# An mLSTM and pooling block on one core: block sums spread over three feature tiles, the first head's loads reordered, and every store to DRAM issued by GpSimd's queue

## The chip, the core and the metric

One core of a Trainium2 chip runs the kernel. The metric is the device time of one execution in microseconds. A run also leaves a profile of one execution, whose span is the time from its first to its last instruction.

Short names: PE is TensorE, PEld its weight loads, DVE VectorE, ACT ScalarE, POOL GpSimd, SP SyncE. SPq and POOLq are the sequencers of SP and POOL, which also issue transfers. L375 is line 375 of the kernel before.

## The reference, cut to what matters

Two layers act on 1024 latent tokens of width 1024; 256 context tokens stand before them. Layer 0 is a bidirectional mLSTM over four heads of 512, layer 1 a grid pooling mixer. Cut to what the change touches:

```
h = modulate(rmsnorm(x, pre_g), shift, scale)       # latent and context
xm, z, og = split(h @ w_in, 3)                      # 2048 features each
xc = silu(short_conv(xm)); q, k = headwise(xc); v = headwise(xm)
hsum = bidir_mlstm(q, k, v, gates)                  # context states first
y = (sigmoid(og) * headnorm(hsum) + skip * xc) * silu(z) @ w_out
x = x + gate * rmsnorm(y)
u, z = split(h2 @ w_in, 2)                          # layer 1
x = x + gate * rmsnorm((pool_diff(u) @ w_pool * scale * silu(z)) @ w_out)
```

All is float32. The kernel makes each product from three matmuls, on a high and a low part of both operands, so each operand needs a split: a copy on ACT for the high part and a subtraction on DVE for the low one.

## The kernel before

**Features (`features`, `token_part`).** Sixteen tiles of 128 features, n = 0 to 15. A tile multiplies one weight tile by three chunks of tokens (512, 512, 256), eight steps of three matmuls each. Each chunk is copied out of PSUM twice on ACT (L373 into the convolution's input, L375 into the high part `xmh`), DVE makes the low part (L376). Then come the convolution (L378 on ACT, L379 and L380 on DVE, L381 on ACT) and its split (L388 ACT, L389 DVE). `token_part(n)` is a generator whose matmuls are put between those of tile n + 1, from its first chunk on; they read `xmh` of tile n. A tile stores `xc` (L383), four pieces of its split (L391, L392), and two pairs of value tiles (L421): nine stores.

**Block sums.** `block_sums` prepares, for k = 0 to 3, four sums of blocks of h for the products that follow. For one k it loads two rows of h (L519), makes four sums on DVE (L522 to L525), and for each of the four sums a split (L529 on ACT, L530 on DVE) and a store (L531). It is a generator with six yields for one k; after each feature tile from n = 2 on, three of its steps are taken (two from n = 10 on), so that one k takes two tiles: loads, sums and one split after the even tile, three splits after the odd one.

**Gates and the z and og products.** One pair of tiles is multiplied plainly, the other pairs by a block scheme of seven products (`strassen`), whose weight sums POOL makes (L575 to L578). `o_done` stores two tiles for each result (L625).

**Heads.** Four heads, eight tiles of 128 tokens each. For each tile `decay` fills tiles with exp (ACT), POOL masks their diagonals (L774, L775), `score_chunk` multiplies three chunks of keys, `weights` normalises, `turn` transposes, `values` multiplies by v (POOL takes a power in it, L814), and `store` writes 128 x 512 to DRAM (L831). Before the first tile L850 to L856 load the first head's keys by chunks (`fetch_x`), the gate rows (`load_gates`, `load_ctx_gates`, two and two transfers) and v (`fetch_v`); `next_q` makes the first queries.

**Output and layer 1.** `product` multiplies by an output weight, `residual` scales, adds and stores (L1009), partly on POOL; layer 1's `pool_tile` stores L1162. The last quarter of the tokens ends with three stores (L1207).

**What sets the order.** Every transfer, load or store, is issued by SP's queue, in order: a store that waits for its data holds the loads behind it. Each engine works through its own list in order, too. PE's order is written out by hand for the features, the z and og products, the output products and layer 1. All other orders are made by a scheduler when the program is built: it takes the instructions in program order as their priority, and plays them through against modelled durations. Buffers come from pools by tag: "S4" has 32 buffers of 4 KB a partition, "T5" 5, "hn" 3, "pt" 6. A tile waits for a free buffer of its tag, and a stored tile's buffer is free when the store has landed.

Of the kernel before, what the change touches and what calls it, by code (L numbers as in the profile page):

```python
# [51 lines left out]
def hybrid_block(ctx: ExitStack, tc: tile.TileContext, xT, ctxT, vecs, w_ada0, w_ada, w_blk, w_krow, blk_mask, w_gate, w_in, b_gate, w_out,  # L52
# [209 lines left out]
    def modulate(src, r, parts, k, j, dst=None):  # L262
        sc, sh = gs0[:, k, j:j + 1], mod0[:, k, 0, j:j + 1]
        V.scalar_tensor_tensor(src, src, sc, r, op0=ALU.mult, op1=ALU.mult)
        if dst is not None:
            nc.sync.dma_start(dst, src)
        for hi, _, c in parts:
            S.activation(hi, src[:, c], AF.Identity, bias=sh)
        for hi, lo, c in parts:
            V.scalar_tensor_tensor(lo, src[:, c], sh, f(hi), op0=ALU.add, op1=ALU.subtract)  # L270
# [87 lines left out]
    def features(n, side):  # L358
        wh, wl = first_w[n] if n < 2 else load_w(w_in[n])
        xp = tl("T5", [P, 1284])  # L360
        for z in (0, 1025, 1282):
            G.memset(xp[:, z:z + 1], 0.0)
        cp = tl("pt", [P, 2, TC], F32R)
        xmh = [tl("S4", [P, T], F32R), cp[:, 0]]
        xml = [tl("S4", [P, T], F32R), cp[:, 1]]
        for ci, (o, w) in enumerate(CHUNKS):
            p = pt_("pa") if n > 1 else ps_[n][ci]
            for k in range(KD if n > 1 else 0):
                mm3(p[:, :w], wh[:, k], wl[:, k], hx(k, ci, 0), hx(k, ci, 1), k == 0, k == KD - 1)
                if n == 2 or k % 2:  # L370
                    next(side, None)
            xo = 1 + o if ci < 2 else 1026
            S.activation(xp[:, xo:xo + w], p[:, :w], AF.Copy)  # L373
            dh, dl = (xmh[0][:, o:o + w], xml[0][:, o:o + w]) if ci < 2 else (xmh[1], xml[1])
            S.activation(dh, p[:, :w], AF.Copy)  # L375
            V.tensor_tensor(dl, xp[:, xo:xo + w], f(dh), op=ALU.subtract)  # L376
        y = tl("T5", [P, 1281])
        S.activation(y, xp[:, 1:1282], AF.Identity, scale=vc("conv_w", 16 + n), bias=vc("conv_b", n))  # L378
        V.scalar_tensor_tensor(y, xp[:, 0:1281], vc("conv_w", n), y, op0=ALU.mult, op1=ALU.add)  # L379
        V.scalar_tensor_tensor(y, xp[:, 2:1283], vc("conv_w", 32 + n), y, op0=ALU.mult, op1=ALU.add)  # L380
        S.activation(y, y, AF.Silu)  # L381
        yl, yc = y[:, 0:T], y[:, 1025:1281]
        nc.sync.dma_start(xc_d[n], yl)  # L383
        cp = tl("pt", [P, 2, TC], F32R)
        xch = [tl("S4", [P, T], F32R), cp[:, 0]]
        xcl = [tl("S4", [P, T], F32R), cp[:, 1]]
        for s_, h_, l_ in ((yl, xch[0], xcl[0]), (yc, xch[1], xcl[1])):
            S.activation(h_, s_, AF.Copy)  # L388
            V.tensor_tensor(l_, s_, f(h_), op=ALU.subtract)  # L389
        for t, dst in ((xch, xh_d), (xcl, xl_d)):  # L390
            nc.sync.dma_start(dst[n, :, 0:T], f(t[0]))  # L391
            nc.sync.dma_start(dst[n, :, T:TA], f(t[1]))  # L392
        return xmh, xml, xch, xcl

    def token_part(n, xmh, xml, xch, xcl):
# [8 lines left out]
        for s0 in (0, 5):  # L404
            vst, vhl = tl("T5", [P, 2, 5, 144]), tl("T5", [P, 2, 5, P], F32R)
            for s in range(s0, s0 + 5):
                yield
                if s < 8:
                    ah, al = xmh[0][:, s * P:(s + 1) * P], xml[0][:, s * P:(s + 1) * P]
                else:  # L410
                    ah, al = xmh[1][:, (s - 8) * P:(s - 7) * P], xml[1][:, (s - 8) * P:(s - 7) * P]
                p = pt_("pb", [P, 2, 144])
                mm(p.rearrange("p a b -> p (a b)"), ah, vv.rearrange("p a b -> p (a b)"), True, False)
                mm(p[:, 0], al, vv[:, 0], False, True)
                S.activation(vst[:, :, s - s0], p, AF.Copy)  # L415
            V.tensor_tensor(vst[:, 0], vst[:, 0], vst[:, 1], op=ALU.add)
            V.tensor_tensor(pre[:, s0:s0 + 5], pre[:, s0:s0 + 5], vst[:, 0, :, P:], op=ALU.add)
            S.activation(vhl[:, 0], vst[:, 0, :, :P], AF.Copy)
            V.tensor_tensor(vhl[:, 1], vst[:, 0, :, :P], f(vhl[:, 0]), op=ALU.subtract)
            for t, dst in ((vhl[:, 0], vh_d), (vhl[:, 1], vl_d)):  # L420
                nc.sync.dma_start(dst[n // 4, :, s0:s0 + 5, (n % 4) * P:(n % 4 + 1) * P], f(t))  # L421
        yield

        gx = gx_all[:, n]
# [13 lines left out]
    def gates():  # L438
# [56 lines left out]
        scans(m_r, mc_r, ALU.max, lambda r, a, b, st: i_r[r, a:b][:, ::st])  # L495
        V.tensor_tensor(i_r[:36, 0:T], i_r[:36, 0:T], b_r[:36], op=ALU.subtract)
        V.tensor_tensor(i_r[:36, T:TA], i_r[:36, T:TA], bc_r[:36], op=ALU.subtract)
        nc.sync.dma_start(a_d, i_r[:36, :])
        V.tensor_tensor(b_r[:36], b_r[:36], m_r[:36], op=ALU.subtract)
        yield  # L500
        nbt.append(small([P, 8, 36], "cst", 1))
# [9 lines left out]
    def block_sums():  # L511
# [4 lines left out]
        for k in range(4):  # L516
            t0, t1 = tl("S4", [P, T]), tl("S4", [P, T])
            for t, kk in ((t0, k), (t1, k + 4)):
                nc.sync.dma_start(t, h_d[kk])  # L519
            yield  # L520
            b11, b12, b21, b22 = t0[:, :512], t0[:, 512:], t1[:, :512], t1[:, 512:]
            V.scalar_tensor_tensor(b22, b22, dsh[:, k], b12, op0=ALU.add, op1=ALU.subtract)  # L522
            V.tensor_tensor(b12, b12, b11, op=ALU.subtract)
# [3 lines left out]
            for j, x in ((2, b11), (3, b22), (1, b12), (4, b21)):  # L527
                t = tl("S4", [P, 2, 512], F32R)
                S.activation(t[:, 0], x, AF.Copy)  # L529
                V.tensor_tensor(t[:, 1], x, f(t[:, 0]), op=ALU.subtract)  # L530
                nc.sync.dma_start(t_d[j - 1, k], f(t))  # L531
                yield

    side, parts, sums = iter(()), [], block_sums()
    with ctx0:
        gate_weights()
        for n in range(KE):
# [76 lines left out]
        def o_done(n, sz, xc, i, hf, t):  # L614
# [7 lines left out]
                nc.sync.dma_start(x, xc_d[n + i, :, hf * 512:hf * 512 + 512])  # L622
            V.scalar_tensor_tensor(x, x, vc("skip", n + i), sz[i][:, hf], op0=ALU.mult, op1=ALU.mult)
            for t_, dst in ((sg, ga_d), (x, gb_d)):
                nc.sync.dma_start(dst[(n + i) // 4, 4 * hf:4 * hf + 4, :, (n + i) % 4].rearrange("t p x -> p t x"),  # L625
                                  t_.rearrange("p (t x) -> p t x", t=4))

        steps = gates()
# [72 lines left out]
                hd.setdefault(part, []).append(t)  # L701

    def load_ctx_gates(h):
        rc = tl("hn", [P, 2, TC])
        for d in range(2):
            nc.sync.dma_start(rc[:, d], a_d[32 * d + h:32 * d + h + 1, T:TA].to_broadcast([P, TC]))
        return rc
# [115 lines left out]
    def store(st, tag="pc"):  # L823
# [4 lines left out]
        ht = tl("hn", [P, 4, P])  # L828
        V.tensor_tensor(ht, p, ab[0], op=ALU.mult)
        V.tensor_tensor(ht, ht, ab[1], op=ALU.add)  # L830
        nc.sync.dma_start(y1_d[4 * h:4 * h + 4, :, ti * P:(ti + 1) * P].rearrange("c p t -> p c t"), ht)  # L831

    BYTES["T5"] = 5120
    phase("ph2")
# [13 lines left out]
            fetch_x(cur["hd"], cur["h"], ci)  # L848

    cur = start_head(0)  # L850
    fetch_x(cur["hd"], 0, 1)
    cur["A"] = make_A(0)
    cur["q"] = next_q(cur, 0)
    cur["R"], cur["rc"] = load_gates(0), load_ctx_gates(0)
    fetch_x(cur["hd"], 0, 2)
    fetch_v(cur["hd"], 0, 0, 5)  # L856
    st_prev = st_now = nxt = None
    for i in range(len(seq) + 1):
# [137 lines left out]
    def residual(yo, rs, o, w, xr, dst, acc2, engs):  # L996
# [5 lines left out]
        for n in range(8):  # L1002
# [3 lines left out]
            if acc2 is not None:  # L1006
                squares(t, acc2, n, w)
            if n % per == per - 1:
                nc.sync.dma_start(dst[:, n - per + 1:n + 1, o:o + w], yo[n // per])  # L1009
            yield STEP_R * w / 512  # L1010

    gg0 = const([P, 8], "gg0")
# [100 lines left out]
    for g in range(4):  # L1113
# [32 lines left out]
        def pool_tile(j):  # L1146
            n = 4 * g + j
            w = load_w(bw_pool[n], 4)
            for hf in range(2):
# [9 lines left out]
                    o = yraw[n // 2, hf][:, n % 2]  # L1159
                V.scalar_tensor_tensor(o, p, vc("pool_scale", n), szs[j][:, s_], op0=ALU.mult, op1=ALU.mult)  # L1160
                if g < 3:
                    nc.sync.dma_start(y2_d[n, :, s_], o)  # L1162

        def box_tile(j):
            d.append(box(ut[j], g, imv))
# [36 lines left out]
    for e, i, n0, n1 in ((V, 0, 0, 4), (G, 1, 2, 4), (V, 1, 0, 2)):  # L1202
# [1 line left out]
        r = rs if e is V else rss  # L1204
        e.tensor_tensor(t, t, r[:, None, :].to_broadcast([P, n1 - n0, 256]), op=ALU.mult)
        e.tensor_tensor(t, t, xr[i][:, n0:n1], op=ALU.add)
        nc.sync.dma_start(outT[:, 4 * i + n0:4 * i + n1, 768:1024], t)  # L1207
    ph["stack"].close()


# [77 lines left out]
```

## Time and profile before

| | before |
|---|---|
| median of 3 runs | 2068.04 us (2063.6 to 2069.58) |
| the profiled execution, its own time | 2062.41 us |
| its span | 2060.7 us |
| mean granted clock of PE | 0.986 |
| PE busy | 1982.7 us, 96% of the span |
| DVE, ACT, POOL busy | 61%, 39%, 14% |
| moved by DMA | 339.47 MB, 165 GB/s over the span |

Busy times do not count the instructions that issue transfers. A wait in the tables below is the idle time of an engine in front of an instruction, with the instruction or transfer that ended it. The granted clock is a share of 2.4 GHz.

### The profile page before, as it was taken

What the parts mean: (1) busy time and instruction counts of PE and PEld (TensorE: products, weight loads), DVE (VectorE), ACT (ScalarE), POOL (GpSimd) and SP (SyncE); (2) the same over time, 40 slices, a digit from 0 to 9 for tenths busy, and PEclk for the clock granted to TensorE, in tenths of its full rate; (3) what the DMA queues carried; (4) which work ended last, traced back from release to release, by engine and by line L of the source; (5) the groups of instructions that cost most, each with busy time, mean ns of one, the idle gap of its engine ahead of it and who ended that gap; (6) DMA issues with size and microseconds to landing.
All of it is one profiled execution on the core that took longest, in us unless ns stands there. A gap on an engine that the chain in (4) does not pass through costs nothing.

```text
span 2060.7 us, 26787 instructions
## 1 busy us (share of the span) xinstructions
PE 1982.7 (96%) x10050; PEld 1668.4 (81%) x10050; DVE 1258.9 (61%) x2092; ACT 809.4 (39%) x1353; POOL 289.5 (14%) x376
## 2 busy tenths in 40 slices
PE   6888889999999999999999999999999999999997
PEld 4777778788888788888888878887888888888897
DVE  4766666787677667667576672544747283744444
ACT  5566666533333432333323322443423132224443
POOL 1000000023322100000000001343000000000275
PEclk9999999999999999999999999999999999999999
DMA  9376776864444854638346334534331312134573
GB/s 364 135 249 219 233 245 215 275 221 128 148 137 125 274 200 139 225 123 275 109 161 213 108 97 138 193 115 164 101 112 51 103 52 87 52 114 137 177 249 127
DMA packets 202499, 339.47 MB, mean 165 GB/s; under 512 B 13021, under 2 KB 116957, under 8 KB 202369
## 3 DMA queue, kind: packets, MB, share of 16 engines
q1 hardware_dynamic: 202368, 337.76, 48.8%
q8 instruction: 78, 1.28, 0.2%
q14 instruction: 53, 0.43, 0.1%
HBM read 234.77 MB, written 102.94 MB: 164 GB/s over the span
## 4 chain that ended last, share of the span: by engine, by line
PE 86%; DVE 5%; DMA 5%; ACT 2%; issue 1%; SPq 0%; POOL 0%; DVEq 0%; ACTq 0%; POOLq 0%
PE pa L136 43%; PE pc L136 34%; PE pb L136 7%; PE pb L796 1%; DMA wr<-in_w_ada_dram 1%; PE pc L827 1%; DMA S<-in_w_ada_dram 1%; DVE S L917 1%; DMA S<-in_ctxT_dram 0%; DMA vl_d<-T 0%; DVE wl L673 0%; DMA T<-in_bw_out_dram 0%; DMA S<-xh_d 0%; DMA cst<-in_w_blk_dram 0%; DVE wl L144 0%
## 5 line engine op out<-in xcount | busy, mean ns | idle before, releaser
L136 PE MATMUL pa<-S,wh 128*128 128x512 f32 (+1 forms) x2448 | 712.7, 376 | 1.7 <-ACT pt L375 1.7
L136 PEld LDWEIGHTS pa<-S,wh 128*128 128x128 f32 x2448 | 439.5, 191 | 72.2 <-ACT pt L375 2.9
L136 PE MATMUL pc<-S,wh 128*128 128x512 f32 (+1 forms) x1664 | 464.7, 365 | 3.2 <-ACT wh L142 2.3
L136 PE MATMUL pa<-S,wl 128*128 128x512 f32 (+1 forms) x1224 | 454.0, 371 | 3.3 <-DVE wl L144 3.3
L136 PEld LDWEIGHTS pc<-S,wh 128*128 128x128 f32 x1664 | 301.5, 189 | 54.6 <-ACT wh L142 2.5
L144 DVE TENSOR_TENSOR wl<-wr,wh 128x1024 fp32r<-128x1024 f32 (+1 forms) x124 | 146.9, 1185 | 267.2 <-ACT wh L142 266.0
L136 PE MATMUL pc<-S,wl 128*128 128x512 f32 (+1 forms) x832 | 302.3, 365 | 1.0 <-DVE wl L144 1.0
L136 PEld LDWEIGHTS pa<-S,wl 128*128 128x128 f32 x1224 | 233.1, 190 | 44.0 <-DVE wl L144 3.7
L142 ACT ACTIVATE wh<-wr 128x1024 fp32r<-128x1024 f32 (+1 forms) x124 | 124.6, 1005 | 358.1 <-PE pa L136 137.0
L136 PE MATMUL pa<-S,S 128*128 128x512 f32 (+1 forms) x1152 | 249.0, 362 | 5.4 <-DMA S<-xh_d 5.0
L136 PE MATMUL pc<-S,pt 128*128 128x512 f32 x960 | 227.5, 391 | 1.4 <-DVE S L736 0.9
L136 PEld LDWEIGHTS pa<-S,S 128*128 128x128 f32 x1152 | 191.7, 190 | 34.8 <-DMA S<-xh_d 5.5
L136 PEld LDWEIGHTS pc<-S,pt 128*128 128x128 f32 x960 | 178.2, 188 | 38.4 <-DVE S L736 1.6
L136 PEld LDWEIGHTS pc<-S,wl 128*128 128x128 f32 x832 | 157.5, 189 | 26.4 <-DVE wl L144 1.8
L798 ACT ACTIVATE pt<-pb 128x512 fp32r<-128x512 f32 (+1 forms) x96 | 47.8, 524 | 211.8 <-PE pb L796 202.7
L985 POOL TENSOR_TENSOR hn<-hn,pt 128x512 f32<-128x512 f32 (+1 forms) x48 | 77.7, 1621 | 308.4 <-ACT pt L984 307.4
L755 DVE SCALAR_TENSOR_TENSOR T<-pa,T 128x256 f32<-128x256 f32 (+3 forms) x184 | 78.1, 453 | 35.9 <-PE pa L136 31.4
L136 PEld LDWEIGHTS pb<-vv,S 128*128 128x128 f32 x256 | 48.3, 194 | 40.3 <-ACT S L375 16.2
L415 ACT ACTIVATE T<-pb 128x288 f32<-128x288 f32 x160 | 62.9, 412 | 43.2 <-PE pb L136 42.7
L585 ACT ACTIVATE wh<-T 128x512 fp32r<-128x512 f32 x70 | 41.2, 626 | 98.3 <-PE pc L136 79.6
L136 PE MATMUL pb<-S,wh 128*128 128x512 f32 x256 | 78.8, 389 | 0.0
L136 PE MATMUL pb<-vv,S 128*128 128x288 f32 (+1 forms) x256 | 50.1, 276 | 27.0 <-ACT S L375 14.5
(323 smaller groups left out, 2340.8 us busy)
## 6 DMA issues: line engine op xcount, KB each, us to landing
wr<-in_bw_in_dram SPq DMA_DIRECT2D x40, 512.0 KB, 3.5
wr<-in_w_in_dram SPq DMA_DIRECT2D x34, 512.0 KB, 4.3
wr<-in_w_ada_dram SPq DMA_DIRECT2D x32, 512.0 KB, 3.8
wr<-in_w_out_dram SPq DMA_DIRECT2D x32, 512.0 KB, 3.6
T<-in_bw_out_dram SPq DMA_DIRECT2D x32, 512.0 KB, 4.7
S<-y_d SPq DMA_DIRECT2D x28, 512.0 KB, 7.5
vh_d<-T SPq DMA_DIRECT2D x32, 320.0 KB, 2.8
vl_d<-T SPq DMA_DIRECT2D x32, 320.0 KB, 3.6
```

The costliest lines, as they stand in the source:

```text
L136: PE.matmul(out, lhsT, rhs, start=start, stop=stop)
L142: S.activation(h, r, AF.Copy)
L144: V.tensor_tensor(l, r, f(h), op=ALU.subtract)
L415: S.activation(vst[:, :, s - s0], p, AF.Copy)
L585: S.activation(hi, a, AF.Copy)
L755: V.scalar_tensor_tensor(W[:, lo + sh:hi + sh], p[:, lo - o:hi - o], 1.0, W[:, lo + sh:hi + sh], op0=ALU.mult, op1=ALU.mult, accum_out=dp[ ...
L796: PE.transpose(p[:, j], st["M"][:, s * P:(s + 1) * P], ident)
L798: S.activation(th[:, :n], p[:, :n], AF.Copy)
L827: PE.transpose(p[:, c], hn[:, c * P:(c + 1) * P], ident)
L917: V.tensor_tensor(b, yraw[kp, hf], f(a), op=ALU.subtract)
L985: G.tensor_tensor(acc, acc, sq, op=ALU.add)
```

## The change

The diff has three parts. All stores to DRAM (306 of them by the loops of the code: 8 of h, 16 + 64 of the convolution's results, 64 value tiles, 1 of gate rows, 16 block sums, 64 gates, 32 + 8 + 24 intermediate results, 9 outputs) are issued by `nc.gpsimd` instead of `nc.sync`; loads stay on SP. `block_sums` yields three times for one k instead of six, and one step is taken after each tile from n = 2 on: loads and sums after one tile, two splits after the next, two after the third. For the first head, all gate rows and keys are loaded ahead of `make_A` and `next_q`, and its context gate rows lie in an "S4" buffer instead of an "hn" one.

```
@@ stores, 14 places, all alike
-            nc.sync.dma_start(dst, src)
+            nc.gpsimd.dma_start(dst, src)
@@ block_sums
             for t, kk in ((t0, k), (t1, k + 4)):
                 nc.sync.dma_start(t, h_d[kk])
-            yield
             b11, b12, b21, b22 = t0[:, :512], t0[:, 512:], t1[:, :512], t1[:, 512:]
...
                 V.tensor_tensor(t[:, 1], x, f(t[:, 0]), op=ALU.subtract)
-                nc.sync.dma_start(t_d[j - 1, k], f(t))
-                yield
+                nc.gpsimd.dma_start(t_d[j - 1, k], f(t))
+                if j in (3, 4):
+                    yield
...
             if n >= 2:
-                for _ in range(3 if n < 10 else 2):
-                    next(sums, None)
+                next(sums, None)
@@ load_ctx_gates
-        rc = tl("hn", [P, 2, TC])
+        rc = tl("hn" if h else "S4", [P, 2, TC])
@@ first head
     cur = start_head(0)
-    fetch_x(cur["hd"], 0, 1)
+    cur["R"], cur["rc"] = load_gates(0), load_ctx_gates(0)
+    finish_x(cur)
     cur["A"] = make_A(0)
     cur["q"] = next_q(cur, 0)
-    cur["R"], cur["rc"] = load_gates(0), load_ctx_gates(0)
-    fetch_x(cur["hd"], 0, 2)
     fetch_v(cur["hd"], 0, 0, 5)
```

## Rows read from the trace of the kernel before

**Rows 1.** The page, its span and part 1: busy time, share, instructions.
```profile
span 2060.7 us, 26787 instructions
...
PE 1982.7 (96%) x10050; PEld 1668.4 (81%) x10050; DVE 1258.9 (61%) x2092; ACT 809.4 (39%) x1353; POOL 289.5 (14%) x376
```

**Rows 2.** Busy time by engine in four stretches; last columns clock, DMA share, GB/s.
```profile
core 0: us, PE busy (x) PEld busy (x) DVE busy (x) ACT busy (x) POOL busy (x), PEclk, DMA share, GB/s
115.20:292.10 176.90, 153.54 (x788) 127.36 (x788) 115.88 (x181) 109.47 (x203) 2.11 (x25) 0.92 0.70 239
309.64:379.72 70.08, 70.08 (x393) 59.81 (x393) 46.44 (x68) 48.98 (x94) 0.49 (x9) 1.00 0.66 211
703.00:723.00 20.00, 14.96 (x71) 12.35 (x69) 10.12 (x22) 12.47 (x23) 2.04 (x7) 0.91 1.04 362
1984.00:2004.00 20.00, 16.92 (x127) 16.52 (x127) 7.11 (x6) 7.21 (x11) 10.29 (x8) 0.92 1.01 352
```

**Rows 3.** PE's waits, whole span: us in total, times, longest us.
```profile
PE pb L136 <- ACT S L375: 14.5, 4, 4.0
...
PE pa L136 <- DMA S<-xh_d: 5.0, 1, 5.0
```

**Rows 4.** Timeline around a feature tile with block sums, 205 to 236 us.
```profile
215.98 0.97 SPq L519 DMA_DIRECT2D S<-h_d  x1
...
222.65 0.75 DVE L522 SCALAR_TENSOR_TENSOR S<-S,dsh,S 128x512 f32<-128x512 f32 x1 [0.17 <-DMA S<-h_d]
...
227.24 0.63 ACT L529 ACTIVATE S<-S 128x512 fp32r<-128x512 f32 x1 [3.49 <-DVE S L524]
227.77 1.07 ACT L375 ACTIVATE S<-pa 128x512 fp32r<-128x512 f32 x2
228.40 0.19 PEld L136 LDWEIGHTS pb<-vv,S 128*128 128x128 f32 x1 [3.98 <-ACT S L375]
228.40 0.40 PE L136 MATMUL pb<-vv,S 128*128 128x288 f32 x1 [3.56 <-ACT S L375]
```

**Rows 5.** Timeline of a feature tile without block sums, 298 to 317 us.
```profile
298.15 0.60 ACT L373 ACTIVATE T<-pa 128x512 f32<-128x512 f32 x1 [1.02 <-PE pa L136]
...
301.93 0.62 ACT L375 ACTIVATE S<-pa 128x512 fp32r<-128x512 f32 x1
...
308.34 0.17 POOL L362 MEMSET T<- 128x1 f32 x3 [18.12 <-DVE vv L402]
...
315.68 0.60 ACT L373 ACTIVATE T<-pa 128x512 f32<-128x512 f32 x1 [1.01 <-PE pa L136]
```

**Rows 6.** Groups by line on DVE, 115.2 to 292.1 us: busy us, mean ns.
```profile
L416 DVE TENSOR_TENSOR T<-T 128x720 f32<-128x720 f32 x16 | 14.4, 903 | 8.4 <-ACT T L415 8.4
...
L530 DVE TENSOR_TENSOR S<-S,S 128x512 fp32r<-128x512 f32 x16 | 10.3, 684 | 0.0
...
L522 DVE SCALAR_TENSOR_TENSOR S<-S,dsh,S 128x512 f32<-128x512 f32 x4 | 3.0, 752 | 1.0 <-DMA vl_d<-T 0.6 <-DMA S<-h_d 0.4
```

**Rows 7.** Groups by line and form on POOL, whole span.
```profile
L577 POOL TENSOR_TENSOR T<-wr,T 128x512 f32<-128x512 f32 x14 | 23.3, 1661 | 145.5 <-DVE wl L586 143.5 <-PE pb L504 2.0
L576 POOL TENSOR_TENSOR T<-T,wr 128x512 f32<-128x512 f32 x14 | 18.6, 1328 | 1.0
```

**Rows 8.** Line 421's issues on SP: duration ns min/median/max, and landing.
```profile
L421 SPq DMA_DIRECT2D vh_d<-T x32: 359/370/1050, 100.1 to 396.2; - x32
...
DMA to landing us min/median/max: 2.4/3.2/9.2
```

**Rows 9.** Timeline at the start of the heads, 700 to 712 us.
```profile
705.14 1.07 ACT L735 ACTIVATE S<-pc 128x512 fp32r<-128x512 f32 x2
...
705.68 0.39 SPq L713 DMA_DIRECT2D S<-a_d  x1
...
708.33 0.67 SPq L686 DMA_DIRECT2D S<-xh_d  x1
...
711.34 0.99 ACT L770 ACTIVATE T<-S,cst 128x128 f32<-128x128 f32 x3 [3.83 <-DMA S<-a_d]
```

**Rows 10.** The chain that ended last, 700 to 724 us: start, us, what.
```profile
708.33 8.92 DMA S<-xh_d
```

**Rows 11.** Timeline in the last output product, 1976 to 2006 us.
```profile
1979.61 7.04 POOL L1005 TENSOR_TENSOR S<-S,S 128x512 f32<-128x512 f32 x4
...
1986.67 0.38 SPq L1009 DMA_DIRECT2D out_dram<-S  x1
...
1988.54 13.01 SPq L140 DMA_DIRECT2D T<-in_bw_out_dram  x7
```

**Rows 12.** Timeline of the last 15 us.
```profile
2053.85 2.61 DVE L1206 TENSOR_TENSOR S<-S,S 128x1024 f32<-128x1024 f32 x2
2054.80 2.05 SPq L1207 DMA_DIRECT2D out_dram<-S  x3
```

**Rows 13.** Timeline of one tile in the heads, 990 to 1026 us.
```profile
1000.99 0.81 DVE L816 TENSOR_SCALAR hn<-pc,mv,rs__1597_9027 128x512 f32<-128x512 f32 x1 [0.73 <-POOL rs__1597_9027 L814]
```

More of the change, by code (lines that the diff above doesn't have):

```diff
@@ L382, in features @@
         yl, yc = y[:, 0:T], y[:, 1025:1281]
-        nc.sync.dma_start(xc_d[n], yl)
+        nc.gpsimd.dma_start(xc_d[n], yl)
         cp = tl("pt", [P, 2, TC], F32R)
@@ L390, in features @@
         for t, dst in ((xch, xh_d), (xcl, xl_d)):
-            nc.sync.dma_start(dst[n, :, 0:T], f(t[0]))
-            nc.sync.dma_start(dst[n, :, T:TA], f(t[1]))
+            nc.gpsimd.dma_start(dst[n, :, 0:T], f(t[0]))
+            nc.gpsimd.dma_start(dst[n, :, T:TA], f(t[1]))
         return xmh, xml, xch, xcl
@@ L420, in token_part @@
             for t, dst in ((vhl[:, 0], vh_d), (vhl[:, 1], vl_d)):
-                nc.sync.dma_start(dst[n // 4, :, s0:s0 + 5, (n % 4) * P:(n % 4 + 1) * P], f(t))
+                nc.gpsimd.dma_start(dst[n // 4, :, s0:s0 + 5, (n % 4) * P:(n % 4 + 1) * P], f(t))
         yield
@@ L497, in gates @@
         V.tensor_tensor(i_r[:36, T:TA], i_r[:36, T:TA], bc_r[:36], op=ALU.subtract)
-        nc.sync.dma_start(a_d, i_r[:36, :])
+        nc.gpsimd.dma_start(a_d, i_r[:36, :])
         V.tensor_tensor(b_r[:36], b_r[:36], m_r[:36], op=ALU.subtract)
@@ L624, in o_done @@
             for t_, dst in ((sg, ga_d), (x, gb_d)):
-                nc.sync.dma_start(dst[(n + i) // 4, 4 * hf:4 * hf + 4, :, (n + i) % 4].rearrange("t p x -> p t x"),
+                nc.gpsimd.dma_start(dst[(n + i) // 4, 4 * hf:4 * hf + 4, :, (n + i) % 4].rearrange("t p x -> p t x"),
                                   t_.rearrange("p (t x) -> p t x", t=4))
@@ L830, in store @@
         V.tensor_tensor(ht, ht, ab[1], op=ALU.add)
-        nc.sync.dma_start(y1_d[4 * h:4 * h + 4, :, ti * P:(ti + 1) * P].rearrange("c p t -> p c t"), ht)
+        nc.gpsimd.dma_start(y1_d[4 * h:4 * h + 4, :, ti * P:(ti + 1) * P].rearrange("c p t -> p c t"), ht)
     BYTES["T5"] = 5120
@@ L1008, in residual @@
             if n % per == per - 1:
-                nc.sync.dma_start(dst[:, n - per + 1:n + 1, o:o + w], yo[n // per])
+                nc.gpsimd.dma_start(dst[:, n - per + 1:n + 1, o:o + w], yo[n // per])
             yield STEP_R * w / 512
@@ L1161, in pool_tile @@
                 if g < 3:
-                    nc.sync.dma_start(y2_d[n, :, s_], o)
+                    nc.gpsimd.dma_start(y2_d[n, :, s_], o)
         def box_tile(j):
@@ L1206, in hybrid_block @@
         e.tensor_tensor(t, t, xr[i][:, n0:n1], op=ALU.add)
-        nc.sync.dma_start(outT[:, 4 * i + n0:4 * i + n1, 768:1024], t)
+        nc.gpsimd.dma_start(outT[:, 4 * i + n0:4 * i + n1, 768:1024], t)
     ph["stack"].close()
```

## The prediction, made before the changed kernel was run

> **What bounds the kernel now.** I read the page's busy times first: PE works 1982.7 of 2060.7 us [rows 1], so at most 78 us of idle PE, and what a lowered clock costs, can be won; work moved off DVE, ACT or SP is worth nothing unless PE waits for it. The second view is the busy time by stretches, to find where those 78 us lie. Three of the stretches touch the change [rows 2]. From 115.20 to 292.10 us (feature tiles 3 to 10, whose stretch holds the block sums) PE is busy 153.54 of 176.90 us at a clock of 0.92; from 309.64 to 379.72 us (four tiles without block sums) it is never idle, at 1.00. At the start of the heads (703 to 723 us) it is idle 5.04 us, and in the last output product (1984 to 2004 us) 3.08 us. The third view, PE's waits, names the causes: four waits, up to 4.0 us, for the copy L375 on ACT, and one of 5.0 us for a load of keys [rows 3]. The timelines then show what stands before each.
>
> **Part 1, block sums.** Four tiles without them take 70.08 us, 17.52 us each; eight at that pace take 140.2 us, and the stretch with block sums takes 176.9: 36.7 us more, about 9.2 for each of the four k [rows 2]. Idle PE is 23.4 us of it; the rest goes with the lowered clock. The cause is a place in ACT's list. In program order the first split (L529) of a k stands ahead of the next tile's first L375. It needs the sum on DVE, which needs rows of h whose second load was issued at 215.98 and for which DVE waits until 222.65. ACT stands idle 3.49 us at L529; L375 comes directly behind it at 227.77, for two chunks at once; PE, in its fixed order, waits for it until 228.40 [rows 4]. In a tile without block sums the same copy starts at 301.93, 3.8 us after its chunk's first copy at 298.15 [rows 5].
>
> The change moves that split one step later, behind the next tile's copies: after one tile come loads and sums only, after the next two splits whose sums are long done. What ACT stood waiting at is no longer ahead of L375. DVE still meets the four sums in line: four of at most 0.752 us, 3.0 us, and it can stand waiting for h there. What hides this is the room of L375 and L376 in a tile: PE wants L375's result near the start of the following tile, which begins at 309.64 [rows 2]; a copy at 301.93 that comes 3 us later leaves some 4 us. Without that cover each of the four k would keep up to 3 us of its 9. Two splits put 2 x 0.684 us on DVE [rows 6], hidden the same way. The load loses its step of lead, but the scheduler used to run loads and sums in one turn anyway, since three steps were taken at once. I take 35 us of gain; the bounds are 36.7 (all of it) and 18 (half stays, because DVE waiting for h passes its delay on).
>
> **Part 2, the first head's loads.** Buffers of tag S4 are handed out in program order. Queries (L735, 705.14) stand before the gate rows and the context keys, so those loads are issued only at 705.68 and 708.33 [rows 9]; ACT waits 3.83 us for the gate rows, and the keys' load lands 8.92 us after its issue, which is the chain [rows 10]. In the new order both stand ahead of the queries and start as buffers of the products before come free. Their one wait for PE, 5.0 us, and the clock of 0.91 behind it (9% of 20 us, 1.8 us) can go: 6.8 us at most. Next in line is v, ten loads still behind the queries, in a stretch whose DMA share is already 1.04 [rows 2]. I take 5; bounds 0 and 6.8.
>
> **Part 3, stores to POOL.** First what it frees. In the last output product SP stood at a store of the output until POOL had finished 7.04 us of residual work; then a load of weights went out at 1988.54, the first of seven back to back, so the buffers had been waiting for it [rows 11]. The idle 3.08 us and 8% of 20 us of clock make 4.7 [rows 2]; on POOL's queue these stores stand behind the work they need, and SP's loads run ahead. I take 4; bounds 0 and 4.7. The Trainium skill (DMA: Bandwidth & Descriptors, Issuing engines are not separate DMA queues) speaks against any such gain: transfers from all queues run on the same engines, and another issuer saves only issue time. By that page this term would be 0 and the sum 4 us worse; the row shows a load held by a waiting store, which is order and not bandwidth.
>
> Then what it costs. The trace has no transfer issued by POOL. From below an issue costs what SP's does, 0.37 us; from above a tensor operation of POOL, 1.33 to 1.66 us [rows 7, 8]. A feature tile issues nine stores and 16 block-sum stores fall on 12 tiles: 10.3 a tile, 3.8 to 17.1 us of its 17.52. Both ends fit, so the sum does not hang on the price. I take about 1 us, between the ends, since no row resembles it. Behind a waiting store now stand POOL's own instructions. In the features that is the memset L362; it starts at 308.34 and its tile's first copy comes at 315.68 [rows 5], so 7 us of later landing (now 3.2 us in the middle, 9.2 at most [rows 8]) are covered. In the z and og stage POOL is idle 143.5 us waiting for buffers of its weight sums [rows 7], so eight stores per pair fit. In the heads DVE waits 0.73 us for POOL's power [rows 13], and a store just ahead would add its issue to that; DVE is not what PE waits for there. I take 2 us for all this; bounds 0 and, with all covers thin, 10.
>
> At the end SP issues three stores in 2.05 us, the last one after DVE's last addition [rows 12]. One issue by POOL in its place adds 0 to 1.3 us; I take 0.7. The stores of h, x1 and layer 1 are read long after, and I cost them at nothing: their cover is that distance, and without it each would cost one landing, 3.2 us.
>
> **The sum**, against the profiled execution's own 2062.4 us: -35 -5 -4 +2 +0.7 = -41.3, so 2021.1. The median of the runs is 2068.0, 5.6 us above that execution, so I forecast 2026 us. The bounds reach from 2012 (all gains, no cost) to 2050 (half of part 1, part 2 alone of the rest, and 3 us of cost, about).
>
> **Rivals.**
> 1. *DVE takes over the gap.* Sums stand early in DVE's list, the loads of h have no lead, and DVE waiting there holds L379 and L376 behind it. For: the load still takes 6.7 us to reach DVE. Against: DVE waited only 0.17 us at it [rows 4]. Half of part 1 is lost: 2044. Chance 0.09.
> 2. *The order does not come out as written.* The scheduler's modelled times may put the copies behind the sums as before, and the gaps stay; then only parts 2 and 3 count, 6 us: 2062, within 0.3% of the median. For: ACT's list is the scheduler's, not the program's. Against: program order is its priority, and the split now stands a tile later. Chance 0.05.
> 3. *POOL's queue becomes the bound of the feature tiles* and the kernel slower. 10.3 issues fill 17.52 us at 1.7 us each; from 2.05 us each, 12 tiles lose the 42 us that all else gains. This would be if an issue costs POOL a tensor operation and also waits out a DVE operation: 1.33 + 0.90 [rows 6, 7] = 2.23, 23.0 us a tile, 65 us over 12 tiles: 2091. For: DVE is busy two thirds of these stretches [rows 2]. Against: most of its operations there are two-input ones, and POOL's own idle is large. Chance 0.10. The Trainium skill (SBUF — State Buffer, Who interferes with whom) bears on it: GpSimd writes the descriptors of its transfers through ports that a DVE copy in a two-port mode locks, and no run here shows that yet.
>
> **How the numbers follow.** Forecast 0.76, between 2012 and 2040; rival 1 0.09; rival 2 0.05; rival 3 0.10. A measurement of this kernel can tell about 0.3%, 6 us, from no change. Faster by more than that: 0.76 + 0.09 = 0.85; within it 0.05; slower 0.10. The range runs from 2010 to 2052: it takes in the bounds and rival 1, and leaves out rival 3, rival 2 and a little of the rest.
>
> **What would show it.** Part 1: tiles 3 to 14 at 17.5 us each, no wait of PE for L375, clock 1.00 from 115 us on; wrong if ACT still stands idle at L529 or DVE at L522. Part 2: gate rows and context keys issued before L735, PE's idle near 710 us gone; v may be late instead. Part 3: no idle of PE near 1999 us; POOL's issues about 1 us each, and in the features fewer than 17 us of them a tile. The forecast is wrong if an issue costs 2 us or more, if PE's idle from 115 to 292 us stays over 12 us, or if POOL's masks and powers in the heads come so late that PE waits for them.

## The result and the profile after

The kernel after takes 2035.42 us (median of 4 runs, 2033.27 to 2037.47), the kernel before 2068.61 us beside it (4 runs, 2063.6 to 2069.58): a ratio of 0.9844, 95% interval 0.9825 to 0.9863, 33 us less. The forecast was 2026 us with a range of 2010 to 2052: sign and range held, and 9 us of the gain did not come.

The page of after, its busy times and its DMA queues (q1 is the queues of SP, q0 those of POOL); it answers to [rows 1]:

```profile
span 2032.8 us, 26908 instructions
...
PE 1970.0 (97%) x10050; PEld 1661.2 (82%) x10050; DVE 1256.6 (62%) x2092; ACT 812.5 (40%) x1357; POOL 500.2 (25%) x682
...
DMA packets 115986, 339.47 MB, mean 167 GB/s; under 512 B 13036, under 2 KB 20716, under 8 KB 115856
...
q1 hardware_dynamic: 85824, 234.80, 34.2%
q0 software_dynamic: 30032, 102.96, 13.7%
```

PE's idle time went from 78 us to 62.8 (2032.8 - 1970.0), and its busy time for the same 10050 matmuls from 1982.7 to 1970.0: a part of the gain is clock. POOL's 306 more instructions are the moved stores, which on POOL count as busy: 210.7 us more, 0.69 us each.

The two profiled executions are 27.9 us of span apart, less than the medians, because the one of before was 6 us faster than its kernel's median. To see where the 27.9 us lie, take the start of the same instruction in both traces. From the third tile on, the third chunk's copy (L375, into `pt`) stands 14 times in the features, so first to last is 13 tiles:

| stretch | before | after | change |
|---|---|---|---|
| start to the first of these copies | 116.9 | 117.4 | +0.5 |
| 13 feature tiles | 262.8 | 232.4 | -30.4 |
| to the first result of the block products | 60.3 | 57.8 | -2.5 |
| to the first normalised head tile | 311.5 | 314.1 | +2.6 |
| heads, to the first copy of layer 1 | 670.9 | 672.5 | +1.6 |
| to the last square of the last product | 626.1 | 624.3 | -1.8 |
| to the end | 12.2 | 14.3 | +2.1 |

The features give more than the whole gain. The other rows say little: a run below (`t_d`, `vh_d` and `vl_d` moved) has the instructions of PE, DVE and ACT in the order of before, and its first four rows still read 120.6, 262.4, 58.3 and 312.8 us. So outside the 13 tiles a difference of 1 to 4 us between two traces needs no cause in the change.

Busy time by engine in the 13 feature tiles, of before and then of after (last columns: PE's clock, DMA share, GB/s); in the fence of after also the start of the heads and the last output product, for [rows 2]:

```profile
116.90:379.70 262.80, 239.44 (x1270) 200.66 (x1269) 172.95 (x263) 168.98 (x315) 2.77 (x37) 0.95 0.69 231
```

```profile
117.40:349.80 232.40, 227.84 (x1270) 193.95 (x1269) 171.12 (x263) 167.15 (x316) 91.44 (x173) 1.00 0.73 261
...
673.00:693.00 20.00, 12.05 (x58) 10.20 (x58) 9.35 (x19) 11.02 (x20) 2.72 (x7) 0.83 1.04 402
1954.00:1974.00 20.00, 20.00 (x169) 20.00 (x167) 9.92 (x8) 9.97 (x15) 16.23 (x15) 1.00 0.96 357
```

With the same 1270 matmul records, idle PE falls from 23.4 to 4.6 us (18.8 won) and busy PE by 11.6 us, as the clock goes from 0.95 to 1.00: here PE's waits were paid for a second time, in the lowered clock behind them. The last output product has lost its idle time. The start of the heads is worse: 7.95 us idle where there were 5.04.

PE's waits over the span of after, for [rows 3]:

```profile
PE pb L136 <- ACT T L415: 10.8, 9, 2.4
PE pa L136 <- ACT S L734: 8.0, 2, 7.8
PE pb L136 <- POOL hn L983: 6.5, 3, 4.8
```

The four waits for L375 are gone, and so is the one for the keys. In its place stands one of 7.8 us for the queries' copy (L734, the L735 of before). Timeline of ACT in a feature tile of after, for [rows 4] (L528 is the split that was L529):

```profile
196.83 0.42 ACT L388 ACTIVATE pt<-T 128x256 fp32r<-128x256 f32 x1
197.14 0.42 ACT L415 ACTIVATE T<-pb 128x288 f32<-128x288 f32 x1
197.43 1.17 ACT L528 ACTIVATE S<-S 128x512 fp32r<-128x512 f32 x2
198.47 0.61 ACT L375 ACTIVATE S<-pa 128x512 fp32r<-128x512 f32 x1
200.18 0.60 ACT L373 ACTIVATE T<-pa 128x512 f32<-128x512 f32 x1 [1.10 <-PE pa L136]
...
201.78 0.71 ACT L415 ACTIVATE T<-pb 128x288 f32<-128x288 f32 x2
...
216.37 1.17 ACT L528 ACTIVATE S<-S 128x512 fp32r<-128x512 f32 x2
...
219.05 0.39 ACT L415 ACTIVATE T<-pb 128x288 f32<-128x288 f32 x1
219.34 0.60 ACT L373 ACTIVATE T<-pa 128x512 f32<-128x512 f32 x1
```

Two splits run with no idle time ahead of them, and the copy follows; the rows from 216.37 on are the next tile, with the other two splits. At the start of the heads the timeline of ACT shows what PE waits for now, for [rows 9]:

```profile
666.97 1.28 ACT L769 ACT_TABLE_LOAD   x1 [3.17 <-DMA S<-a_d]
...
669.27 1.28 ACT L615 ACT_TABLE_LOAD   x1
...
671.22 1.28 ACT L771 ACT_TABLE_LOAD   x1
...
678.44 1.69 ACT L772 ACTIVATE T<-S,cst 128x256 f32<-128x256 f32 x4
680.14 1.28 ACT L615 ACT_TABLE_LOAD   x1
681.44 1.15 ACT L615 ACTIVATE hn<-pt 128x512 f32<-128x512 f32 x2
682.49 1.55 ACT L734 ACTIVATE S<-pc 128x512 fp32r<-128x512 f32 x3
```

The gate rows come early, as the change wants. ACT's list now has the exponentials of several tiles (L768 to L772) and four table loads, 666.97 to 681.44, ahead of the last sigmoid (L615) and of the queries' copy.

### The profile page after: what moved, and what is told of

Its sections match the earlier page's. It is cut to its first block, busy times and chain, and to the rows that moved or that the text cites. A ratio compares the mean times of both kernels' runs of the same rounds, so it can differ in the third digit from the quotient of the medians.

```text
span 2032.8 us, 26908 instructions
## 1 busy us (share of the span) xinstructions
PE 1970.0 (97%) x10050; PEld 1661.2 (82%) x10050; DVE 1256.6 (62%) x2092; ACT 812.5 (40%) x1357; POOL 500.2 (25%) x682
## 3 DMA queue, kind: packets, MB, share of 16 engines
q1 hardware_dynamic: 85824, 234.80, 34.2%
q0 software_dynamic: 30032, 102.96, 13.7%
## 4 chain that ended last, share of the span: by engine, by line
PE 89%; DMA 3%; ACT 3%; DVE 2%; POOL 2%; issue 1%; SPq 0%; POOLq 0%; DVEq 0%; ACTq 0%
PE pa L136 45%; PE pc L136 34%; PE pb L136 7%; PE pb L795 2%; POOL hn L983 1%; PE pc L826 1%; DVE S L915 1%; DMA S<-in_w_ada_dram 1%; DMA S<-in_ctxT_dram 0%; DMA cst<-in_w_blk_dram 0%; DMA S<-a_d 0%; DMA wr<-in_w_ada_dram 0%; DMA S<-in_xT_dram 0%; POOL S L1003 0%; ACT wh L142 0%
## 5 line engine op out<-in xcount | busy, mean ns | idle before, releaser
L136 PE MATMUL pa<-S,wh 128*128 128x512 f32 (+1 forms) x2448 | 703.5, 372 | 0.0
L136 PEld LDWEIGHTS pa<-S,wh 128*128 128x128 f32 x2448 | 433.9, 189 | 67.7
L983 POOL TENSOR_TENSOR hn<-hn,pt 128x512 f32<-128x512 f32 (+1 forms) x48 | 75.7, 1578 | 284.4 <-ACT pt L982 283.5
L754 DVE SCALAR_TENSOR_TENSOR T<-pa,T 128x256 f32<-128x256 f32 (+3 forms) x184 | 78.2, 455 | 32.7 <-PE pa L136 31.8
L415 ACT ACTIVATE T<-pb 128x288 f32<-128x288 f32 x160 | 62.5, 413 | 40.5 <-PE pb L136 33.0
L808 DVE BATCH_NORM_STATS2 st<-pc 128x6 f32<-128x512 f32 x32 | 22.4, 699 | 86.6 <-PE pc L136 86.5
L144 DVE TENSOR_TENSOR wl<-T,wh 128x1024 fp32r<-128x1024 f32 x32 | 45.7, 1428 | 43.4 <-ACT wh L142 43.3
```

Of the source, the lines that this page charges most:

```text
L136: PE.matmul(out, lhsT, rhs, start=start, stop=stop)
L144: V.tensor_tensor(l, r, f(h), op=ALU.subtract)
L754: V.scalar_tensor_tensor(W[:, lo + sh:hi + sh], p[:, lo - o:hi - o], 1.0, W[:, lo + sh:hi + sh], op0=ALU.mult, op1=ALU.mult, accum_out=dp[ ...
L808: V.bn_stats(b6, pv)
L983: G.tensor_tensor(acc, acc, sq, op=ALU.add)
```

## The experiments

The numbers of lines in runs built on the kernel before are its own. "Features" is the 13-tile stretch of the table above.

### One part at a time

Three kernels are the kernel before with one of the diff's parts alone (in the edits three dots stand for lines not shown); the fourth is the kernel after without the second part.

**Part 1 alone (block sums):**

```diff
-            yield
...
-                yield
+                if j in (3, 4):
+                    yield
-                for _ in range(3 if n < 10 else 2):
-                    next(sums, None)
+                next(sums, None)
```

> The kernel before with the block sums spread over three tiles, nothing else. If the split's place in ACT's list makes the four gaps, features 3 to 10 run at 17.5 us a tile or nearly so, and the kernel is 30 to 35 us below before (2033 to 2039, ratio 0.983 to 0.986). If the gaps are made by stores that hold SP's loads of h (rival), most of the 36.7 us stays and the kernel is within 10 us of before.

Measured: 2037.1 us, ratio 0.9858 (0.9843 to 0.9873), about 28 us less than before (2065.34 us in these runs). Features 232.8 us: part 1 by itself gives all that the features give.

**Part 2 alone (the first head's loads):**

```diff
-        rc = tl("hn", [P, 2, TC])
+        rc = tl("hn" if h else "S4", [P, 2, TC])
...
-    fetch_x(cur["hd"], 0, 1)
+    cur["R"], cur["rc"] = load_gates(0), load_ctx_gates(0)
+    finish_x(cur)
     cur["A"] = make_A(0)
     cur["q"] = next_q(cur, 0)
-    cur["R"], cur["rc"] = load_gates(0), load_ctx_gates(0)
-    fetch_x(cur["hd"], 0, 2)
```

> The kernel before with the first head's loads reordered, nothing else. The changed kernel's trace shows PE idle about 8 us at the start of the heads behind the copy of the queries on ACT, so the reorder should cost here what it cost there: 1 to 4 us slower than before, or no change that can be told. The prediction had taken 5 us of gain.

Measured: 2067.33 us, ratio 1.0007 (0.9997 to 1.0017): nothing. PE's wait of 5.0 us for the keys is gone, and one of 7.5 us for the queries' copy has come.

**Part 3 alone (all stores on GpSimd's queue):** every store to DRAM, as in the line

```diff
-        nc.sync.dma_start(xc_d[n], yl)
+        nc.gpsimd.dma_start(xc_d[n], yl)
...
```

> The kernel before with all stores issued by POOL, nothing else. If the gaps are the split's place, they stay: PE idle about 23 us between tiles 3 and 10; 5 us are won in the last output product, 2 lost at the end and about 3 at the start of layer 1, so within 4 us of before. If SP's held loads make the gaps (rival), they shrink, and 15 us or more are won.

Measured: 2045.33 us, ratio 0.9902 (0.9887 to 0.9917): 20 us less, where I had expected next to nothing. Features 243.0 us, 19.8 less than before. Three of the four waits of PE for L375 are gone, 3.2 us are left in one. So parts 1 and 3 remove the same gaps: 28 and 20 us alone, 31 to 33 together, and with part 1 in place part 3 does nothing more for the features (232.8 and 232.4).

**After without part 2:** the second diff undone.

> The changed kernel with the first head's loads in the old order. If the reorder costs 2.6 us in the changed kernel, as the times of its stages say, this one is 1 to 5 us below it, 2030 to 2034, with PE's 5 us wait for context keys back and the 8 us wait for the queries' copy gone. If the reorder helps, it is up to 7 us above it.

Measured: 2034.01 us, ratio 0.9845 (0.9831 to 0.986), against 0.9844 for after: the second part is worth nothing here either. PE's wait for the keys is back, 6.6 us, and the one for the queries' copy is gone.

### Why moving stores closes the gaps

My first theory was the queue: on SP the loads of h stand behind stores that wait for their data; without the stores they come early.

```diff
-                nc.sync.dma_start(t, h_d[kk])
+                nc.gpsimd.dma_start(t, h_d[kk])
```

> The kernel before with one thing changed: the eight loads of the block sums' input (h_d) are issued on GpSimd's queue, which has no stores in this kernel, so they stand behind no store that waits for its data. Theory: the 20 us that the stores' move alone gave came from these loads, which SyncE's queue held behind waiting stores, so that the sums came late and ScalarE stood at their first split (14.2 us in 4 waits before, 3.1 us in 1 with the stores moved): 2045 to 2055 us, with that idle time below 5 us. Rival: the gain came from the stores themselves (their landing, the buffers they give back, or the DMA packets), and the loads' place does nothing: 2063 to 2069 us.

Measured: 2061.41 us, ratio 0.9983 (0.9973 to 0.9992), features 260.7 us, about 2 us less than before. ACT still stands 12.6 us in four waits for the sums. The time lies just below the rival's range and far from the theory's: the theory fell. Timeline of one of them, POOL's issue, then DVE, then ACT:

```profile
156.55 1.14 POOL L519 DMA_DIRECT2D S<-h_d  x2 [0.34 <-issue]
...
175.68 0.74 DVE L522 SCALAR_TENSOR_TENSOR S<-S,dsh,S 128x512 f32<-128x512 f32 x1
...
179.15 1.55 DVE L379 SCALAR_TENSOR_TENSOR T<-T,vec,T 128x1281 f32<-128x1281 f32 x1
180.62 0.74 DVE L524 SCALAR_TENSOR_TENSOR S<-S,mod,S 128x512 f32<-128x512 f32 x1
...
181.39 0.63 ACT L529 ACTIVATE S<-S 128x512 fp32r<-128x512 f32 x1 [3.14 <-DVE S L524]
```

The two rows of h are issued 19 us ahead of the first sum (they land in 3.8 to 6.7 us), and it changes little: the third sum (L524), for which ACT waits, still stands behind the convolution (L379) in DVE's list. So the second theory was the lists: with fewer stores in SP's list the scheduler, which builds each engine's order against modelled times, places the sums earlier. Two groups of the features' stores tell the theories apart, since moving one leaves the order of PE, ACT and DVE as it was, and moving the other does not.

**Block sums' and value rows' stores on GpSimd:** `t_d`, `vh_d` and `vl_d`, 80 issues by the loops of the code (the expectation counts too few).

```diff
-                nc.sync.dma_start(t_d[j - 1, k], f(t))
+                nc.gpsimd.dma_start(t_d[j - 1, k], f(t))
...
```

> The kernel before with two groups of the feature stage's stores issued by GpSimd, the block sums' (t_d) and the value rows' (vh_d, vl_d), 56 issues; the others stay on SyncE. The order in which VectorE and ScalarE get their instructions is that of the kernel before. Theory: the 20 us of the stores' move come through that order (the planner puts VectorE's three sums ahead of the convolution once SyncE's list is free), so nothing is won here: 2061 to 2066 us, with ScalarE's four waits for the sums at 12 to 15 us. Rival: they come from what SyncE's queue does on the chip (loads behind stores that wait, buffers that come back sooner); these are the stores that wait longest, so half or more of the 20 us is won: 2045 to 2056 us.

Measured: 2066.15 us, ratio 1.0002 (0.9992 to 1.0012); features 262.4 us; ACT's four waits for the sums 14.5 us. One of them, DVE and then ACT:

```profile
182.19 0.75 DVE L522 SCALAR_TENSOR_TENSOR S<-S,dsh,S 128x512 f32<-128x512 f32 x1 [0.50 <-DMA vl_d<-T]
...
184.53 1.55 DVE L379 SCALAR_TENSOR_TENSOR T<-T,vec,T 128x1281 f32<-128x1281 f32 x1
186.00 0.75 DVE L524 SCALAR_TENSOR_TENSOR S<-S,mod,S 128x512 f32<-128x512 f32 x1
...
186.78 0.63 ACT L529 ACTIVATE S<-S 128x512 fp32r<-128x512 f32 x1 [3.83 <-DVE S L524]
```

**The other stores on GpSimd:** `xc_d`, `xh_d` and `xl_d`, 80 issues too, five a tile.

```diff
-        nc.sync.dma_start(xc_d[n], yl)
+        nc.gpsimd.dma_start(xc_d[n], yl)
...
```

> The kernel before with the other feature stores alone issued by GpSimd (xc_d, xh_d, xl_d: 50 issues, five a tile). Here the planner's order changes: VectorE's three sums stand ahead of the convolution in the list from the second block sum on. Theory (the order does it): most of the 20 us is won, 2044 to 2051 us, with ScalarE's waits for the sums at one or none. Rival (SyncE's queue on the chip): these stores wait little, so at most 8 us are won: 2056 to 2066 us.

Measured: 2046.94 us, ratio 0.9904 (0.9885 to 0.9922): all of what the move of all stores gave; features 242.7 us; ACT waits once for the sums, 3.1 us. The second block sum of this kernel, DVE and then ACT:

```profile
175.86 0.75 DVE L522 SCALAR_TENSOR_TENSOR S<-S,dsh,S 128x512 f32<-128x512 f32 x1
...
178.44 0.75 DVE L524 SCALAR_TENSOR_TENSOR S<-S,mod,S 128x512 f32<-128x512 f32 x1
...
185.14 1.56 DVE L379 SCALAR_TENSOR_TENSOR T<-T,vec,T 128x1281 f32<-128x1281 f32 x1
...
180.33 0.63 ACT L529 ACTIVATE S<-S 128x512 fp32r<-128x512 f32 x1
180.85 1.09 ACT L375 ACTIVATE S<-pa 128x512 fp32r<-128x512 f32 x2
```

All sums run ahead of the convolution, and the copy L375 starts 0.8 us after the third chunk's copy (180.07), where it starts 6.7 us after it (180.60) in the run before. The gain goes with the place of the third sum in DVE's list: won where it moves ahead of the convolution (this run and part 3 alone), not won where it stays behind it (the two others). The same holds inside this run: for its first block sum the third sum still stands behind the convolution, and that tile takes 25.9 us (26.4 in before); the three others have the new order and take 20.1 to 20.2 us (26.6 to 26.8). Queue and order still changed together in this run. Why the scheduler's modelled times turn on these five stores a tile, and whether the same order with all stores on SP would be as fast, was not tried.

### The start of the heads

Two kernels are the kernel after with one of the second part's two moves taken back.

**Gate rows late**, against the kernel after:

```diff
-    cur["R"], cur["rc"] = load_gates(0), load_ctx_gates(0)
     finish_x(cur)
     cur["A"] = make_A(0)
     cur["q"] = next_q(cur, 0)
+    cur["R"], cur["rc"] = load_gates(0), load_ctx_gates(0)
```

> The kernel after with the first head's gate rows loaded behind the query step again, as in the kernel before, and the third key chunk kept early. Theory: the gate rows that come early let ScalarE's list take the exponentials of five tiles ahead of the queries' copy, and that makes TensorE's wait of 7.8 us on the copy; with the rows late again that wait goes and so does the wait of 6.3 us on the key chunk: 2026 to 2030 us. Rival: the early key chunk is what delays the queries: the wait of 7.8 us stays, 2034 to 2037 us.

Measured: 2031.58 us, ratio 0.9844 (0.9829 to 0.9859), before 2064.52 us in these runs. The copy's wait is gone, as the theory said, but PE waits 5.4 us for DVE's L754 instead, and the time is above what was expected.

**Key chunk late**, against the kernel after:

```diff
+    fetch_x(cur["hd"], 0, 1)
     cur["R"], cur["rc"] = load_gates(0), load_ctx_gates(0)
-    finish_x(cur)
     cur["A"] = make_A(0)
     cur["q"] = next_q(cur, 0)
+    fetch_x(cur["hd"], 0, 2)
```

> The kernel after with the gate rows early, as in it, and the third key chunk behind the query step again. Theory: the wait of 7.8 us on the queries' copy stays, and the key chunk may wait beside it: 2034 to 2042 us. Rival (the early key chunk is to blame): the copy's wait goes, 2027 to 2031 us.

Measured: 2033.86 us, ratio 0.9852 (0.9837 to 0.9867). The time lies just below the theory's range, but the reason does not hold: the copy's wait shrank to 2.1 us with the gate rows early. ACT's timeline shows why:

```profile
673.36 0.98 ACT L769 ACTIVATE T<-S,cst 128x128 f32<-128x128 f32 x3
674.25 0.58 ACT L734 ACTIVATE S<-pc 128x512 fp32r<-128x512 f32 x1
...
676.67 0.58 ACT L734 ACTIVATE S<-pc 128x512 fp32r<-128x512 f32 x1
677.27 1.28 ACT L771 ACT_TABLE_LOAD   x1
678.57 1.15 ACT L771 ACTIVATE T<-S,cst 128x1024 f32<-128x1024 f32 x1
```

Here the first two copies stand ahead of most of the exponentials. So early gate rows alone do not make the wait; both loads early do, by the place of the copy in ACT's list. In neither kernel does a smaller wait show in the time. The first normalised head tile comes 310.1 and 311.0 us after the block products' first result (314.1 in after), and the heads then take 676.4 and 676.2 us (672.5): what was won goes again. PE's clock is 0.87 there in two windows of 13 us (1190 to 1203, 1320 to 1333) where after has 0.97 or more. Why it falls in these kernels and not in after stays open.

### What POOL's queue can carry

Every store of the features is cut in three:

```diff
-                nc.gpsimd.dma_start(t_d[j - 1, k], f(t))
+                [nc.gpsimd.dma_start(t_d[j - 1, k][:, b_, a_:z_], f(t[:, b_, a_:z_]))
+                 for b_, a_, z_ in ((0, 0, 512), (1, 0, 256), (1, 256, 512))]
...
```

> The kernel after with every store of the feature stage cut in three, so that GpSimd issues 27 a tile (and 4 to 6 more with block sums) in place of 9 (and 1.3 to 2). At the durations of the trace of after (0.55 us for the projected rows, 0.87 us for the value rows) that is 20 to 22 us a tile against the 17.5 us that TensorE needs. Theory: GpSimd's queue has room for the change's own stores and binds only beyond 17.5 us a tile, so here the feature stage grows by 2.5 to 4.5 us a tile, 20 to 36 us in all. Rival: an issue of a third of the data takes a third of the time, and nothing grows: the stage stays within 4 us of after's. Another: GpSimd is already near its limit, and the stage grows by more than 40 us.

Measured: 2104.64 us (one execution). Features 284.4 us, 52.0 more than after: 4.0 us a tile, inside the 2.5 to 4.5 expected of one. The 20 to 36 us "in all" counted eight tiles where there are thirteen; in all, 52.0 is also more than the 40 us of the second rival, so the total does not separate the two. The scheduler's orders also change with the cut, so part of it may be theirs: PE's waits there are for L415, 41.4 us in 14. POOL's groups, lines and forms apart, of this kernel from 115 to 460 us (busy us, mean ns, idle before and its cause), and its busy times in one stretch:

```profile
L421 POOL DMA_DIRECT2D vh_d<-T x93 | 62.0, 669 | 20.6 <-ACT T L418 14.3 <-ACT T L415 4.1 <-issue 1.8
...
L383 POOL DMA_DIRECT2D xc_d<-T x42 | 22.7, 545 | 26.9 <-ACT T L415 16.1 <-ACT T L381 9.1 <-ACT S L375 1.5
...
200.00:300.00 100.00, 88.56 (x475) 73.92 (x474) 66.38 (x103) 62.11 (x117) 86.36 (x160) 0.97 0.63 216
```

The same groups of after, 115 to 350 us:

```profile
L421 POOL DMA_DIRECT2D vl_d<-T x26 | 22.7, 875 | 8.2 <-DVE T L419 7.7 <-issue 0.3
...
...
L383 POOL DMA_DIRECT2D xc_d<-T x13 | 7.4, 566 | 56.8 <-ACT T L415 56.8
```

A third of the data costs 545 ns to issue where the whole costs 566. With three issues in place of one POOL is 86% busy and PE stands idle 11.4 us in these 100.

### Stores back on SyncE, and the combination

The kernel after with two groups of stores on SP again:

```diff
-                nc.gpsimd.dma_start(dst[:, n - per + 1:n + 1, o:o + w], yo[n // per])
+                (nc.sync if dst is x1_d else nc.gpsimd).dma_start(dst[:, n - per + 1:n + 1, o:o + w], yo[n // per])
...
-        nc.gpsimd.dma_start(outT[:, 4 * i + n0:4 * i + n1, 768:1024], t)
+        nc.sync.dma_start(outT[:, 4 * i + n0:4 * i + n1, 768:1024], t)
```

> The kernel after with two groups of stores back on SyncE: the first layer's residual rows (x1) and the three stores that end the program. Theory: GpSimd stood 9.3 us at the first x1 store, with the squares that free layer 1's buffers behind it, and its three last issues end later than SyncE's did: the start of layer 1 gets back about 1.6 us of TensorE's idle time and the end 1.3 to 2 us, 2031 to 2034 us. Rival: on SyncE the x1 stores hold up loads of layer 1 and the end is set by the landing alone: 2035 to 2038 us.

Measured: 2027.74 us, ratio 0.9824 (0.9808 to 0.9841), the fastest here, against 0.9844 for after (the two intervals overlap, so I read the gain in the stretches). POOL at the start of layer 1 in after:

```profile
1401.36 0.75 POOL L1007 DMA_DIRECT2D x_d<-S  x1 [9.29 <-DVE S L1003]
1402.29 4.69 POOL L983 TENSOR_TENSOR hn<-hn,pt 128x512 f32<-128x512 f32 x1 [0.18 <-ACT pt L982]
```

and in this kernel:

```profile
1401.15 12.62 POOL L983 TENSOR_TENSOR hn<-hn,pt 128x512 f32<-128x512 f32 x7 [10.22 <-ACT pt L982]
```

PE's wait of 4.8 us for the squares (L983) is gone; one of 3.3 us for DVE's weight split has come, 1.5 us better on balance, and 1380 to 1440 us has 1.6 us more of busy PE. But this cannot be put to the queue of the x1 stores. PE's waits for the squares over the span of part 1 alone, which has all stores on SP (one of 3.6 us at the start of layer 1):

```profile
PE pb L136 <- POOL hn L984: 4.0, 2, 3.6
```

And the two kernels of the section on the heads, which have the x1 stores on POOL, have no wait for the squares there, but one of 3.9 us for the weight split. The lists of DVE and ACT differ between these kernels, and the wait goes with them. From the last square to the end 12.1 us pass, where it was 12.2 before the change and 14.3 in after.

This diff and the one of the late key chunk together:

> The kernel after with the x1 stores and the last three stores on SyncE again, and with the third key chunk behind the query step while the gate rows stay early. Theory: the two gains stand in different stretches (start of layer 1 and end: 4 to 7 us by the run that made only that change; start of the heads: PE's wait of 7.8 us down to 2.1 us, of which the run that made only that change kept 1 to 2 us in the time), so they add: 2023 to 2028 us, against about 2034 for the kernel after. Rival: the wait at the heads comes back later in the list, and only the stores count: 2027 to 2031 us.

Measured: 2030.76 us, ratio 0.9829 (0.9814 to 0.9844): the gains do not add. Against the run above, the stretch of the head loads and block products gives 2.5 us in the trace (311.5 for 314.0), the heads take them back (673.3 for 670.4), and PE waits 3.6 us for the squares at the start of layer 1, with the x1 stores on SP. By its median the best version here is after with these two groups of stores on SP.

## Why the prediction was right, and where not

**What bounds the kernel: right.** The cause in ACT's list, the four gaps of 9 us and their clock were read rightly; the part that removes them carries the result.

**Part 1, taken at 35: right in kind, measured 30.0 alone** (262.8 to 232.8 us), inside its bounds. Thirteen tiles at the 17.52 us of [rows 2] would take 227.8; they take 232.4 in after, and the 4.6 us left are idle PE: four waits for L415, 1.14 us each, one in each of the four tiles that take 18.9 to 19.0 us (the others take 17.6 or less). At the start of such a tile the four sums run on DVE, and in it the first two splits on ACT. The splits' time alone is not the cause: the next tile has two splits in the same place of ACT's list and no wait. What differs is the sums, and in ACT's list L373, which stands 1.10 us for PE, comes ahead of the L415 that PE wants (200.18, 201.78), where it comes behind it in the next tile (219.34, 219.05). The mis-sized term is the cover: the text took the sums and the splits for hidden in the room of L375 and L376, and some 1.4 of each 9 us stay. Which of the two differences makes them was not tried. DVE has no wait at its first sum, so rival 1 did not come. Rival 2 did not come for this part, but what it rests on, that the lists are the scheduler's, is what the account of parts 2 and 3 turns on.

**Part 2, taken at 5: wrong, measured 0.** The failed step is "Next in line is v". The next thing late was the queries' copy, because loads that come early let the scheduler put work that needs them ahead of work that PE needs. Every order tried leaves one wait or another: keys 6.6 us, copy 7.8, weighting 5.4, copy 2.1; none differs in time by more than its interval.

**Part 3 in the last output product, taken at 4: right where it looked.** The stretch that stood idle 3.08 us at a clock of 0.92 is busy all 20 us at 1.00 [rows 2, 11]. The rule against it (the Trainium skill, DMA: Bandwidth & Descriptors, Issuing engines are not separate DMA queues) would have given 0 for this term. Here the wait goes with the queue of the output stores. From PE's waits over the span of before:

```profile
PE pc L136 <- ACT wh L142: 2.3, 1, 2.3
```

This wait for a weight copy in the last output product stands at 2.1 to 2.5 us in all six kernels with the output stores on SP, and in none of the eight with them on POOL. It was worth the 3 us of idle and the clock in this stretch; the whole stretch from layer 1 to the last square shows 1.8 of it. What the term missed is that the same part alone closes three of the four gaps in the features, 20 us; in the sum that is hidden, since part 1 takes the same gaps.

**POOL's costs, taken at 2, and the end at 0.7: the first not measured apart, the second low.** The x1 stores were costed at nothing as being read long after. With them on POOL, PE waits 4.8 us for the squares behind them in after; but PE waits for these squares with the stores on SP too (3.6 us), and in two kernels with them on POOL it does not, so no run here gives their price. The end costs 2.1 us, beyond its bound of 1.3. Timeline of the end of after, for [rows 12]:

```profile
2023.85 2.61 DVE L1204 TENSOR_TENSOR S<-S,S 128x1024 f32<-128x1024 f32 x2
...
2026.15 1.47 POOL L1205 DMA_DIRECT2D out_dram<-S  x2 [0.32 <-DVE S L1204]
```

The last issue ends 1.2 us after the last addition, where it was 0.4: that is about the 0.7 of the text. The trace ends 5.2 us after the last issue, where it was 3.8 (span end less 2056.85): the landing, which the term left out, is the larger part. Over all kernels it is 4.7 to 5.4 us with these stores on POOL and 3.7 to 4.2 on SP, but 5.3 in one kernel on SP, so the queue may not be its only cause.

**The price of an issue, taken at 1 us: 0.69**, in the features 0.67, or 7 of 17.5 us a tile. It lies between SP's price and a tensor operation's [rows 7, 8], nearer the first. Rival 3 needed 2.05 and was far off. With the stores cut in three the issues take 18.7 us a tile (262.3 us over 14 tiles) and the kernel is slower, as rival 3 has it, but with other lists too. The Trainium skill (SBUF — State Buffer, Who interferes with whom) has descriptor writes of GpSimd locked by two-port copies of DVE. With DVE busy 171 of 232 us the 64 issues of L421 last 855 to 922 ns, so none waited long; but nearly all that DVE does there has two inputs and is no copy, so no run here tests the lock.

**The sum.** Forecast -41.3 us, measured -27.9 in span: 4.6 are part 1's (30.4 for 35), 7.6 the start of the heads (+2.6 for -5), the rest small terms of both signs. By the medians 33.2 us were won. After without part 2 has 314.0 us in that stretch, so the 2.6 cannot be laid to part 2; what they are stays open, and a run with the lists of before has 1.4 of them. The prediction's bound of 2012 is lower than its terms give: 36.7 + 6.8 + 4.7 = 48.2 us below 2068.0 is 2019.8.

## What to carry to other kernels

When a scheduler writes the lists, moving a store or a load to another queue can also change the order of the other engines: compare the lists before putting a gain to the queue. Two parts that close the same gap don't add, so test each alone before summing. And before a store's new queue is priced from a wait that came or went, look for the same wait in kernels where that store did not move.

## What was not expected of the hardware

The price of an issue on POOL hangs on its form and hardly on its size: 0.53 to 0.57 us for rows of 256 to 1024 columns, 0.54 for a third of them, 0.87 for value rows in five pieces and 0.67 for one or two of these.

The same 103 MB of stores are 116544 packets when SP issues them (202368 less the 85824 that are left) and 30032 when POOL does, 0.88 and 3.4 KB each. The stores did not land sooner: value rows 4.7 us in the middle, against 2.8.

A wait of PE of 3 to 4 us in the features was followed by a lower clock (0.74 to 0.77 over the 13 us around it, in before), so that 18.8 us of idle time removed were worth 30. The four waits of 1.14 us left in after stand in a stretch at 1.00.
